# One inverse for four head pairs, recurrences moved beside the projections, and SiLU and GELU as activation functions, in a hybrid block kernel

## The chip, the cores and the metric

The kernel runs on one core of a Trainium2 chip. The metric is the device time of one execution in microseconds; the time of a kernel is the median over its runs.

## The reference

One layer of a decoder trunk, followed by an RMSNorm. x is (1024, 2048), all in float32.

```python
h = rmsnorm(x, ln_g)
proj = h @ w_in                                   # 2048 x 6672, split into eleven segments
out_a = gelu(g_u) * (tril(W_s) layernorm(gelu(g_v)) + b) * silu(g_z)   # 4 groups, chunks of 128
q, k, v = split(silu(causal_conv4([d_q, d_k, d_v])))                   # 8 heads x 128
q, k = l2norm(q) / sqrt(128), l2norm(k)
g = -exp(a_log) * softplus(d_a + dt_bias); beta = sigmoid(d_b)
o = gated_delta_rule(q, k, v, g, beta)            # S_t = a_t (I - b_t k_t k_t^T) S_{t-1} + b_t k_t v_t^T ; o_t = S_t^T q_t
out_b = rmsnorm(o, dn_norm_g) * silu(d_z)
mk, mv = split(rmsnorm(mem) @ w_mem_kv)           # 256 memory tokens, 4 heads
out_c = softmax(c_q mk^T / sqrt(128)) mv * silu(c_z)
y = rmsnorm(x + concat(out_a, out_b, out_c) @ w_out, final_g)
```

The delta rule is computed in chunks; each chunk needs the inverse of a unit lower triangular matrix (I + A).

## The kernel before

**Precision.** A float32 product is made of three matmuls (`triple`): each operand is split into a high part (`hi`, a rounding copy on ScalarE) and a low part (`lo`, a subtraction on VectorE), and hi·hi, hi·lo and lo·hi are accumulated. `split_to` does a split; one weight piece is 128x512, and most splits after the first stage take 128x1024.

**Stages.** After the memory keys and values come the *straight* projections of q, k and v of heads 0 to 3 (`project`, one 128-wide column at a time into one of two accumulator banks): all twelve columns for the first half of the sequence (512 tokens, `hf` 0), then, with the activations reloaded (`refill`), the same twelve for the second half. The remaining columns of `w_in` are made in five *pairs* of 512-wide column blocks (`blocks(0)` to `blocks(4)`, through `project_pair` and `seven`), each with seven block products instead of eight: (q, k of heads 4 to 7), (gates of both sets of heads), (v of heads 4 to 7 and gMLP v), (gMLP u and its gate), (attention gate and query). A product fills four banks (`wide`), in the order 2, 1, 6, 5, 3, 7, 4; each bank is emptied by a copy or an addition. Last come two pairs for the output projection (`out_pair`).

**The delta rule for a pair of heads and a half.** `front` runs two convolutions per head (`conv`: copy the bank to one of three buffers `xr`, three VectorE steps, Tanh) and `qk` (norms, decays, the products for `gt` and `ai`). `blocks_out` writes the 32x32 diagonal blocks of `gt` to DRAM; `inverse` loads them, inverts all of them by 31 dependent steps of two VectorE instructions, and writes the results (`tdr`, `udr`) on ScalarE's DMA queue. `levels` combines the blocks into the full inverse `ut`; `values` convolves v; `back` runs four `scan_step`s and `heads_out`, which leaves the output of heads 0 to 3 in DRAM (`od`). For heads 0 to 3 this is done pair by pair, each of the four with an inverse of its own on 32 partitions: the recurrence of pair 0 and the first half runs in the second half of the straight projections, the next one too, and the last two beside the first pair. For heads 4 to 7 the fronts run beside the second pair and leave q, k, kd, ai (`late_d`) and `gt` (`gt_d`) in DRAM, one inverse on 128 partitions does all four, and `front_late` loads them again for the recurrences, beside the fourth pair and after.

**Order.** All instructions are recorded in a `Plan` and then put in order by a simulation of the engines: an instruction has a class (`rank`, smaller is sooner; 5 if nothing is said, 9 for the large matmuls), an estimated cost, and is issued on its engine when its estimated inputs are ready. The order on each engine and queue is then fixed. Large weight loads, stores and reloads all go through SP's queue.

**What the change touches.** `w_parts` keeps the low parts of eight of the twelve columns in DRAM (`low_d`) in the first half and loads them in the second; `tanh_gate` makes SiLU as (tanh(x/2) + 1) · x with the factor one half put into other constants; `gelu2` makes GELU from Square, Tanh and two VectorE steps; `gate`, `gate_late`, `gmlp_gate` and `attn_gate` apply SiLU to the gate columns, `spatial` and `gmlp` apply GELU. `spatial` takes its values through one bank, `hand`.

Of the kernel before, what the change touches and what calls it, by code (L numbers as in the profile page):

```python
# [9 lines left out]
F32 = mybir.dt.float32  # L10
# [28 lines left out]
GELU_C = math.sqrt(2.0 / math.pi)  # L39
GELU_A = 0.044715  # L40
# [8 lines left out]
class Op:  # L49
    __slots__ = ("eng", "fn", "args", "kw", "cls", "idx", "cost", "lat", "nbytes", "lock", "n", "succ", "ready", "at",  # L50
                 "lead", "tail")
# [11 lines left out]
class Plan:  # L63
# [5 lines left out]
    SWITCH = 250.0  # L69

# [63 lines left out]
    def add(self, eng, name, fn, args, kw):  # L134
        o = Op()
        o.eng, o.fn, o.args, o.kw, o.cls, o.idx = eng, fn, args, kw, self.cls, len(self.ops)
        o.succ, o.n, o.ready = [], 0, 0.0
        outs, ins = [], []
# [83 lines left out]
    def issue(self):  # L222
# [4 lines left out]
        dma = beside = 0.0  # L227
        for o in self.ops:
# [55 lines left out]
def kernel(  # L284
# [377 lines left out]
    V.tensor_scalar(col2[:, 0:8], pt[:, 96:104], 0.25, None, op0=ALU.mult)  # L662
    V.tensor_scalar(col2[:, 8:9], pt[:, 104:105], 0.5, None, op0=ALU.mult)
# [10 lines left out]
    halo = C([P, 24, 3], "halo")  # L674
# [10 lines left out]
    V.tensor_scalar(bsb, bsb, 0.25, None, op0=ALU.mult)  # L685
# [23 lines left out]
    late_d = [[[DT([P, HT], f"late{hf}_{h}_{i}") for i in range(4)] for h in range(NJ)] for hf in range(2)]  # L709
    gt_d = [[DT([P, 2 * HT], f"gtd{hf}_{p}") for p in range(NJ // 2)] for hf in range(2)]  # L710
# [60 lines left out]
    scs = [C([P, 12, NT, NH], f"sc{hf}") for hf in range(2)]  # L771
# [8 lines left out]
    def decays(hf, a):  # L780
# [6 lines left out]
        beta, gg, gc, egl, edk, ngb = (sc[:, i] for i in range(6))  # L787
        w0, w1, w2, w3, w4, egc = (sc[:, i] for i in range(6, 12))
# [42 lines left out]
    low_d, todo = {}, []  # L831
# [59 lines left out]
    def conv(which, h, hf, o, a=None):  # L891
# [3 lines left out]
        if h < NJ:  # L895
# [4 lines left out]
            with rank(1):  # L900
                S.copy(xr[:, 0:3], halo[:, ct])
                S.copy(xr[:, 3:], a)
                if hf == 0:
                    S.copy(halo[:, ct], xr[:, HT:])
                S.activation(o, xr[:, 3:], AF.Copy, scale=w[3])
# [21 lines left out]
    def qk(h, hf, q, k, hs, gt):  # L927

        beta, edk, ngc = (scs[hf][:, i] for i in (0, 4, 6))
        bank = over(scan_banks) if h >= NJ or (h >= NJ - 2 and hf == 1) else tpb  # L930
# [52 lines left out]
    def inverse(gdrs, n, cls):  # L983
# [8 lines left out]
        tmp = (y1 if nr == 32 else y2)[0:nr].rearrange("p c m -> p (c m)")  # L992
# [148 lines left out]
    def front(p, hf, first=(None, None)):  # L1141
# [4 lines left out]
        for i, h in enumerate(hp):  # L1146
# [9 lines left out]
            if h >= NJ:  # L1156
                kd, ai, _ = rest[-1]
                V.tensor_copy(late_hs[:, hf, h - NJ], hs[:, 0:5:4])
                for d, t in zip(late_d[hf][h - NJ], (q, k, kd, ai)):
                    Q.dma_start(d if t.ndim == 2 else tok(d), t)  # L1160
        gdr = blocks_out(gt, f"{hf}{p}")
        if p >= NJ // 2:
            Q.dma_start(gt_d[hf][p - NJ // 2].rearrange("p (h t i) -> p h t i", h=2, i=P), gt)
            return gdr
        return hf, hp, gt, qs, ks, hss, rest, gdr

    def front_late(p, hf, inv):
# [3 lines left out]
        Q.dma_start(gt, gt_d[hf][p - NJ // 2])  # L1171
        qs, ks, hss, rest = [], [], [], []
        for h in hp:
            hss.append(ring["hs"]())
            V.tensor_copy(hss[-1][:, 0:5:4], late_hs[:, hf, h - NJ])
            q, k, kd, ai = (ring[t]() for t in ("qT", "kT", "kd", "ai"))
            for d, t in zip(late_d[hf][h - NJ], (q, k, kd, ai)):
# [3 lines left out]
            rest.append((tok(kd), tok(ai), tok(ring["vs"]())))  # L1181
        return hf, hp, gt.rearrange("p (h t i) -> p h t i", h=2, i=P), qs, ks, hss, rest, inv

    def values(hf, hp, gt, qs, ks, hss, rest, inv):
        for i, h in enumerate(hp):
            v = ring["tn"]()
            conv(2, h, hf, v)
            bank = work() if h >= NJ else scan_banks[i] if h >= NJ - 2 and hf == 1 else tpb()
            by_token(rest[i][2], to_tokens((v, bank))[0], hss[i][:, 4])

    def inverted(n, *states):
        return [(*s[:-1], i) for s, i in zip(states, inverse([s[-1] for s in states], n, 3))]

    def back(hf, hp, gt, qs, ks, hss, rest, inv, ut=None):
        ut = ut or levels(gt, *inv)
# [5 lines left out]
    late_hs = C([P, 2, NJ, 2, NT], "lhs")  # L1201
# [582 lines left out]
```

## Time and profile before

| | |
|---|---|
| median of three runs | 1662.21 us (1661.67 to 1664.04) |
| the profiled execution | 1668.24 us, span 1666.5 us |
| instructions | 26200 |
| DMA | 419.50 MB, mean 252 GB/s |

The span is the time from the first to the last instruction of the profiled execution; the execution's own time is a little longer. Every instruction is recorded through one helper, so the profile gives one line, L280, for all, and groups are told apart by the tiles they write and read. PE is TensorE's matmuls, PEld its weight loads, DVE is VectorE, ACT ScalarE, POOL GpSimd, SP the queue that issues most transfers. `acc` are the banks of the large products, `dn` those of everything else. A matmul's recorded duration overlaps with the next one's, so the rate is read from the starts.

### The profile page before, as it was taken

What the parts mean: (1) busy time and instruction counts of PE and PEld (TensorE: products, weight loads), DVE (VectorE), ACT (ScalarE), POOL (GpSimd) and SP (SyncE); (2) the same over time, 40 slices, a digit from 0 to 9 for tenths busy, and PEclk for the clock granted to TensorE, in tenths of its full rate; (3) what the DMA queues carried; (4) which work ended last, traced back from release to release, by engine and by line L of the source; (5) the groups of instructions that cost most, each with busy time, mean ns of one, the idle gap of its engine ahead of it and who ended that gap; (6) DMA issues with size and microseconds to landing.
All of it is one profiled execution on the core that took longest, in us unless ns stands there. A gap on an engine that the chain in (4) does not pass through costs nothing.

```text
span 1666.5 us, 26200 instructions
## 1 busy us (share of the span) xinstructions
PE 1629.0 (98%) x8570; PEld 1361.7 (82%) x8570; DVE 1322.0 (79%) x2288; ACT 1024.0 (61%) x2235; POOL 133.3 (8%) x171
## 2 busy tenths in 40 slices
PE   8999999899999999999999998999999999999997
PEld 6888887787888888888888887888888888888886
DVE  4865787675887969889999997978767897788875
ACT  5957673575746446876777445776666774345445
POOL 0000200111201000110203001000000000000001
PEclk9999999999999999999999998999999999999999
DMA  7878888685887786679978976898877879689746
GB/s 248 240 236 269 272 282 252 178 255 151 274 260 244 245 269 204 194 256 310 310 234 279 298 222 195 257 309 276 264 249 259 259 265 332 234 274 308 227 138 241
DMA packets 317170, 419.50 MB, mean 252 GB/s; under 512 B 58285, under 2 KB 138854, under 8 KB 317034
## 3 DMA queue, kind: packets, MB, share of 16 engines
q1 hardware_dynamic: 304834, 410.48, 76.4%
q10 hardware_dynamic: 10088, 4.21, 1.0%
q0 software_dynamic: 2112, 3.15, 0.7%
q8 instruction: 67, 1.10, 0.3%
q14 instruction: 69, 0.57, 0.1%
HBM read 334.33 MB, written 82.87 MB: 250 GB/s over the span
## 4 chain that ended last, share of the span: by engine, by line
PE 75%; DMA 6%; DVE 5%; ACT 2%; issue 1%; SPq 1%; ACTq 0%; POOLq 0%; POOL 0%; DVEq 0%
PE acc L280 56%; PE dn L280 18%; DMA wraw<-in_w_in_dram 2%; DVE alo L280 1%; DVE y L280 1%; DMA y<-in_w_in_dram 1%; DVE wlo L280 1%; SPq L280 1%; ACT whi L280 0%; ACT ahi L280 0%; DMA late<-kd 0%; ACTq L280 0%; DMA xr<-pd 0%; DVE zl L280 0%; DVE kT L280 0%
## 5 line engine op out<-in xcount | busy, mean ns | idle before, releaser
L280 PE MATMUL acc<-ahi,whi 128*128 128x512 f32 (+1 forms) x1152 | 454.9, 395 | 13.2 <-ACT xr L280 9.2
L280 PE MATMUL acc<-alo,whi 128*128 128x512 f32 (+1 forms) x1152 | 453.5, 394 | 0.0
L280 PE MATMUL acc<-ahi,wlo 128*128 128x512 f32 (+1 forms) x1152 | 452.2, 394 | 0.2 <-DVE wlo L280 0.2
L280 PEld LDWEIGHTS acc<-ahi,whi 128*128 128x128 f32 x1152 | 218.9, 190 | 57.6 <-ACT xr L280 10.3
L280 PEld LDWEIGHTS acc<-ahi,wlo 128*128 128x128 f32 x1152 | 218.9, 190 | 42.2 <-DVE wlo L280 0.6
L280 PEld LDWEIGHTS acc<-alo,whi 128*128 128x128 f32 x1152 | 218.9, 190 | 40.9
L280 PE MATMUL acc<-ahi,zh 128*128 128x512 f32 x736 | 233.4, 394 | 0.0
L280 ACT CAST whi<-wraw 128x512 fp32r<-128x512 f32 (+1 forms) x170 | 137.2, 808 | 110.2 <-PE acc L280 70.3
L280 DVE TENSOR_TENSOR alo<-raws,ahi 128x1024 fp32r<-128x1024 f32 x131 | 160.1, 1223 | 36.5 <-ACT ahi L280 36.2
L280 ACT CAST ahi<-raws 128x1024 fp32r<-128x1024 f32 x131 | 137.4, 1050 | 74.0 <-PE dn L280 28.2
L280 DVE TENSOR_TENSOR wlo<-wraw,whi 128x1024 fp32r<-128x1024 f32 (+1 forms) x138 | 134.0, 972 | 40.9 <-ACT whi L280 35.5
L280 PEld LDWEIGHTS acc<-ahi,zh 128*128 128x128 f32 x736 | 136.9, 188 | 26.8
L280 PE MATMUL acc<-ahi,zl 128*128 128x512 f32 x368 | 145.1, 394 | 0.0
L280 DVE TENSOR_TENSOR ahi<-y,ahi 128x1024 fp32r<-128x1024 f32 x65 | 79.2, 1219 | 20.9 <-ACT ahi L280 20.9
L280 ACT CAST ahi<-y 128x1024 fp32r<-128x1024 f32 x65 | 68.2, 1050 | 30.7 <-PE acc L280 15.6
L280 PEld LDWEIGHTS acc<-ahi,zl 128*128 128x128 f32 x368 | 69.2, 188 | 13.4
L280 ACT CAST zh<-wraw 128x1024 fp32r<-128x1024 f32 x36 | 37.8, 1050 | 57.3 <-PE acc L280 27.2
L280 POOL TENSOR_TENSOR small<-small,mhalf 128x1 f32<-128x1 f32 x26 | 20.0, 773 | 635.8 <-DVE small L280 619.2
L280 POOL TENSOR_TENSOR hs<-hs,mhalf 128x4 f32<-128x4 f32 x32 | 50.8, 1591 | 236.7 <-DVE hs L280 236.6
L280 PE MATMUL dn<-wlo,ahi 128*128 128x512 f32 x152 | 59.0, 389 | 0.0
L280 PE MATMUL dn<-whi,alo 128*128 128x512 f32 x152 | 59.0, 389 | 0.0
L280 PE MATMUL dn<-whi,ahi 128*128 128x512 f32 x152 | 58.8, 389 | 0.0
(398 smaller groups left out, 3227.5 us busy)
## 6 DMA issues: line engine op xcount, KB each, us to landing
wraw<-in_w_in_dram SPq DMA_DIRECT2D x268, 256.0 KB, 4.1
raws<-sd SPq DMA_DIRECT2D x148, 256.0 KB, 3.7
y<-in_w_in_dram SPq DMA_DIRECT2D x92, 256.0 KB, 4.6
y<-sd SPq DMA_DIRECT2D x77, 256.0 KB, 4.0
wraw<-in_w_out_dram SPq DMA_DIRECT2D x64, 256.0 KB, 4.6
raws<-h0d SPq DMA_DIRECT2D x54, 256.0 KB, 4.3
y<-in_w_out_dram SPq DMA_DIRECT2D x33, 256.0 KB, 4.2
low<-wlo SPq DMA_DIRECT2D x32, 256.0 KB, 4.8
```

What stands on the lines that cost most here:

```text
L280: o.fn(*o.args, **o.kw)
```

## The change

Heads 0 to 3 are now treated as heads 4 to 7 were: fronts first, q, k, kd, ai and also vs to DRAM, one inverse on 128 partitions for all four pair-halves, and the four recurrences beside `blocks(0)`. v of heads 0 to 3 is convolved by `early_values` right after the fronts of each half. The low parts are no longer stored; every piece is split where it is used. SiLU and GELU are single activations, with the constants adapted, and the plan knows three activation tables: a switch is priced at 1.5 us, and an activation of another table counts as 1.5 classes later. The buffers `vks`, `vts` and `tmp` change places.

```diff
+    TABLES = {AF.Exp: "exp", AF.Silu: "silu", AF.Gelu_apprx_tanh: "gelu"}
+    TABLE_LOAD = 1500.0
+    STAY = 1.5
...
-            head = self.ops[heapq.heappop(now[e])[1]]
+            if e == "act":
+                other = [(c + self.STAY * (self.ops[i].table not in (None, table)), i, c) for c, i in now[e]]
+                _, i, c = min(other)
+                now[e].remove((c, i))
+                heapq.heapify(now[e])
+                head = self.ops[i]
+            else:
+                head = self.ops[heapq.heappop(now[e])[1]]
             for o in (head, *head.tail):
                 t = max(t, free[e])
+                if o.table not in (None, table):
+                    t, table = t + self.TABLE_LOAD, o.table
...
-    def tanh_gate(a, o, ts):
-
-        t = ts()
+    def silu(a):
         with rank(1):
-            S.activation(t, a, AF.Tanh, scale=0.5)
-            V.scalar_tensor_tensor(o, t, 1.0, a, op0=ALU.add, op1=ALU.mult)
-
-    def gelu2(a, o, ts):
-
-        t = ts()
+            S.activation(a, a, AF.Silu)
+
+    def gelu(a, o):
         with rank(1):
-            if o is not a:
-                S.copy(o, a)
-            S.activation(t, a, AF.Square)
-        V.scalar_tensor_tensor(t, t, 1.0 / GELU_A, o, op0=ALU.add, op1=ALU.mult)
-        S.activation(t, t, AF.Tanh, scale=GELU_A * GELU_C)
-        V.scalar_tensor_tensor(o, t, 1.0, o, op0=ALU.add, op1=ALU.mult)
+            S.activation(o, a, AF.Gelu_apprx_tanh)
...
     def w_parts(c0, kp):
 
         src = w_in[kp * KP * P : (kp + 1) * KP * P, c0 : c0 + P].rearrange("(k p) c -> p k c", p=P)
-        raw = raw_piece(src)
-        if (c0, kp) in low_d:
-            hi, lo = whi(), wlo()
-            with rank(2):
-                S.copy(hi, raw)
-            with rank(4):
-                Q.dma_start(lo.bitcast(F32), low_d[c0, kp])
-        else:
-            hi, lo = split_piece(raw)
-            if (c0 - C_Q) % DW < 2 * P and c0 < C_DV:
-                return [tok(hi), tok(lo)]
-            low_d[c0, kp] = DT([P, HT], f"low{c0}_{kp}")
-            with rank(6):
-                Q.dma_start(low_d[c0, kp], lo.bitcast(F32))
-        return [tok(hi), tok(lo)]
+        return [tok(t) for t in split_piece(raw_piece(src))]
...
+    def early_values(h, hf):
+
+        v, vs = ring["tn"](), tok(ring["vs"]())
+        conv(2, h, hf, v)
+        by_token(vs, to_tokens((v, tpb()))[0], late_hs[:, hf, h, 1])
+        Q.dma_start(tok(late_d[hf][h][4]), vs)
...
-            q, k, kd, ai = (ring[t]() for t in ("qT", "kT", "kd", "ai"))
-            for d, t in zip(late_d[hf][h - NJ], (q, k, kd, ai)):
+            q, k, kd, ai, vs = (ring[t]() for t in ("qT", "kT", "kd", "ai", "vs"))
+            for d, t in zip(late_d[hf][h], (q, k, kd, ai, vs)):
                 Q.dma_start(t, d)
...
-    state = front(0, 0, (first, None))
-    for u in ring["ut"].bufs:
-        G.memset(u, 0.0)
-    (state,) = inverted("00", state)
-    (ahead,) = inverted("01", front(1, 0))
-    values(*state)
-    values(*ahead)
-    back(*state)
+    gdrs = [front(0, 0, (first, None)), front(1, 0)]
+    for h in range(NJ):
+        early_values(h, 0)
...
-    (state,) = inverted("10", front(0, 1, first))
-    back(*ahead)
-    ut = levels(state[2], *state[-1])
-    values(*state)
-    (ahead,) = inverted("11", front(1, 1))
-    back(*state, ut)
-    values(*ahead)
-    back(*ahead)
+    gdrs += [front(0, 1, first), front(1, 1)]
+    with rank(3):
+        early_inv = inverse(gdrs, "early", 3)
+    for h in range(NJ):
+        early_values(h, 1)
+    for u in ring["ut"].bufs:
+        G.memset(u, 0.0)
...
+    def backs(ps, inv):
+        for hf in range(2):
+            for p in ps:
+                state = front_late(p, hf, inv[hf * 2 + p % 2])
+                ut = levels(state[2], *state[-1])
+                if p >= NJ // 2:
+                    values(*state)
+                back(*state, ut)
+
+    with rank(2.6):
+        backs(range(NJ // 2), early_inv)
     blocks(0, to_conv(0), to_conv(1))
...
     def gate(hf, t, y):
-        tanh_gate(y, y, et)
+        silu(y)
...
-    vts = over(vs01 + ring["E"].bufs)
-    vks = [*halves(ring["gt"]()), steps, states[:, 0:HT]]
+    vts = over(vs01 + [steps, states[:, 0:HT]])
+    vks = [t for u in ring["ut"].bufs for t in halves(u)]
```

More of the change, by code (lines that the diff above doesn't have):

```diff
@@ L137, in add @@
         o.succ, o.n, o.ready = [], 0, 0.0
+        o.table = self.TABLES.get(args[2]) if eng == "act" and len(args) > 2 else None
         outs, ins = [], []
@@ L227, in issue @@
         dma = beside = 0.0
+        table = "exp"
         for o in self.ops:
@@ L786, in decays @@
         sc = scs[hf]
[L787 to L788 removed]
+        beta, gg, gc, egl, edk, ngb, w0 = (sc[:, i] for i in range(7))
+        w1, w2, w3, w4, egc = (sct[:, i] for i in range(5))
         tp = tpb()
@@ L929, in qk @@
         beta, edk, ngc = (scs[hf][:, i] for i in (0, 4, 6))
-        bank = over(scan_banks) if h >= NJ or (h >= NJ - 2 and hf == 1) else tpb
+        bank = over(scan_banks) if h >= NJ else tpb
         qt, kt = to_tokens((q, bank()), (k, bank()))
@@ L1187, in values, with back @@
             conv(2, h, hf, v)
[L1188 to L1195, printed above, removed]
+            by_token(rest[i][2], to_tokens((v, work()))[0], hss[i][:, 4])
+    def back(hf, hp, gt, qs, ks, hss, rest, inv, ut):
         for tt in range(NT):
@@ L1545 @@
     blocks(2, to_conv(2), spatial, dest=lambda hf, t: vks[t])
+    for u in ring["ut"].bufs:
+        G.memset(u, 0.0)
     with rank(2.6):
-        for hf in range(2):
-            for p in range(NJ // 2, NJ):
-                state = front_late(p, hf, late_inv[hf * 2 + p - NJ // 2])
-                ut = levels(state[2], *state[-1])
-                values(*state)
-                back(*state, ut)
+        backs(range(NJ // 2, NJ), late_inv)
     def both(c, j, hf, t, y):
@@ L1639, in attend @@
                 PE.matmul(d, mv[h][:, 1, sl], pT[m][0], start=False, stop=m == 1)
-            S.activation(y, d, AF.Copy, scale=0.5)
+            S.copy(y, d)
             both(1, NG + h, hf, h, y)
     def attn_gate(hf, h, y):
-        tanh_gate(y, y, et)
+        silu(y)
         both(1, NG + h, hf, h, y)
```

60 lines of the change are left out of this document (27 added, 33 removed).

## The prediction

> **What bounds the kernel now.** I read the page first, then TensorE by stage, then TensorE's waits, then the timeline at each wait. From the page:
>
> ```profile
> span 1666.5 us, 26200 instructions
> ...
> PE 1629.0 (98%) x8570; PEld 1361.7 (82%) x8570; DVE 1322.0 (79%) x2288; ACT 1024.0 (61%) x2235; POOL 133.3 (8%) x171
> ```
>
> TensorE is busy in all but 37.5 us of the span, and the change neither adds nor removes a matmul or a transpose. So the change can win only idle time and matmuls run at a lower clock, and lose only by making more of them. Next is the view by stage: columns are the stretch, then busy time of PE, PEld, DVE, ACT and POOL, the granted clock, DMA share and GB/s. The stretches are the first half of the sequence for heads 0 to 3, the second half (in two parts), and the five column pairs.
>
> ```profile
> 84.00:252.00 168.00, 167.88 (x842) 140.55 (x841) 121.38 (x258) 113.36 (x314) 17.43 (x22) 1.00 0.86 265
> 252.00:336.00 84.00, 76.98 (x460) 63.89 (x459) 57.67 (x156) 39.62 (x116) 8.31 (x11) 0.96 0.73 213
> 336.00:426.00 90.00, 86.09 (x517) 72.54 (x516) 57.85 (x143) 58.55 (x173) 13.58 (x15) 0.98 0.67 204
> 426.00:604.00 178.00, 176.34 (x948) 146.79 (x946) 153.38 (x269) 100.71 (x201) 15.81 (x18) 1.00 0.81 259
> 604.00:777.00 173.00, 171.37 (x881) 142.85 (x876) 146.41 (x224) 120.62 (x268) 15.56 (x18) 1.00 0.73 241
> 777.00:941.00 164.00, 162.75 (x771) 134.90 (x770) 150.37 (x252) 114.79 (x247) 30.05 (x33) 1.00 0.86 274
> 941.00:1144.00 203.00, 198.55 (x1206) 166.75 (x1205) 170.85 (x286) 120.93 (x244) 14.11 (x21) 0.97 0.80 253
> 1144.00:1342.00 198.00, 198.00 (x1108) 167.87 (x1108) 155.87 (x255) 134.04 (x305) 7.24 (x8) 1.00 0.80 264
> ```
>
> Three stretches lose something a change here can reach: 252 to 426 (7.02 + 3.91 us idle, clock 0.96 and 0.98) and 941 to 1144 (4.45 us idle, clock 0.97). The other rows lose under 2 us each, and the remaining 17 us of the 37.5 lie before 84 and after 1342, where nothing changes. In TensorE's waits the largest is this one (total, times, longest):
>
> ```profile
> PE acc L280 <- ACT xr L280: 9.2, 3, 3.9
> ```
>
> TensorE cannot start a new weight column because both accumulator banks wait for ScalarE's copy into `xr`. The timelines of TensorE, ScalarE and VectorE around two of the three:
>
> ```profile
> 322.47 0.79 PE L280 MATMUL acc<-ahi,whi 128*128 128x512 f32 x1 [3.69 <-ACT xr L280]
> ...
> 329.08 0.40 PE L280 MATMUL acc<-alo,whi 128*128 128x512 f32 x1
> 329.32 0.39 PE L280 MATMUL acc<-ahi,wlo 128*128 128x512 f32 x1
> ```
>
> ```profile
> 413.25 0.50 PE L280 MATMUL acc<-ahi,whi 128*128 128x512 f32 x1 [3.91 <-ACT xr L280]
> ```
>
> ```profile
> 319.33 0.19 ACT L280 COPY xr<-halo 128x3 f32<-128x3 f32 x1 [1.98 <-DVE kT L280]
> ```
>
> ```profile
> 318.56 0.73 DVE L280 SCALAR_TENSOR_TENSOR kT<-xr,cw,kT 128x512 f32<-128x512 f32 x1
> 319.22 0.35 DVE L280 TENSOR_TENSOR inv<-inv,y 32x207 f32<-32x207 f32 x1
> ```
>
> The copy needs one of three `xr` buffers. They are held by convolutions, whose VectorE steps alternate with the steps of an inverse and of a recurrence (ranks 3 and 1 against the convolution's 5). That is the place where this kernel loses most after its start.
>
> **The stalls of the second half.** The two parts hold 10.93 us of idle time and, by the clock, 0.04 x 76.98 + 0.02 x 86.09 = 4.8 us of slowed matmuls: 15.7 us. The third `xr` wait, near 259 (9.2 less 3.69 and 3.91, so 1.6 us), falls at the change of halves, where weights and activations are reloaded; I count it as staying. That leaves 14.1 us. What is late next there is the same as at 259, a weight piece on its way from DRAM. In the new order no inverse and no recurrence stands beside the q and k columns at all; one inverse remains, beside the v columns of the second half or the start of the first pair. Bounds: all 14.1 us go, or that inverse makes a stall like the one at 413 (3.91 us and the 1.7 us of clock in its part, 5.6) again. I take half of it: 14.1 less 2.8, **-11.3 us**.
>
> **The inverses themselves.** Five chains become two, each of the same 31 steps of two instructions:
>
> ```profile
> L280 DVE TENSOR_TENSOR y<-inv,inv 32x31 f32<-32x31 f32 (+25 forms) x155 | 51.6, 333 | 1.9
> L280 DVE TENSOR_TENSOR inv<-inv,y 32x31 f32<-32x31 f32 (+25 forms) x155 | 51.5, 332 | 1.9
> ...
> L280 DVE SCALAR_TENSOR_TENSOR y<-et,y 128x512 f32<-128x512 f32 x40 | 27.2, 695 | 2.2 <-ACT et L280 2.1
> ...
> L280 ACT COPY y<-acc 128x512 f32<-128x512 f32 x72 | 41.9, 584 | 12.3 <-PE acc L280 12.0
> ...
> L280 ACT ACTIVATE et<-y 128x512 f32<-128x512 f32 x40 | 24.8, 631 | 10.7 <-DVE y L280 10.4
> ...
> L280 DVE TENSOR_TENSOR wlo<-kT,whi 128x512 fp32r<-128x512 f32 x14 | 9.6, 688 | 6.7 <-ACT whi L280 4.9 <-PE acc L280 1.9
> ```
>
> (51.6 + 51.5) x 3/5 = 61.9 us leave VectorE; it is worth only what the stalls above are worth, so nothing more is counted. What the combined inverse adds is its end: eight writes in a row on ScalarE's queue, where single ones stood before. The late inverse shows the price:
>
> ```profile
> 1000.33 4.13 ACTq L280 DMA_DIRECT2D tdrlate<-inv  x4
> ...
> 1004.81 5.26 ACTq L280 DMA_DIRECT2D udrlate<-inv  x4
> ```
>
> ```profile
> 1012.79 0.50 PE L280 MATMUL acc<-ahi,whi 128*128 128x512 f32 x1 [1.48 <-ACT y L280]
> ...
> 1015.80 2.08 PE L280 MATMUL dn<-wsT,el 128*128 128x128 f32 x8 [2.03 <-ACT et L280]
> ```
>
> ScalarE issues for 9.4 us; queued behind the issues are its casts of the next operands and the bank copies, and soon after TensorE waits 1.48 us for bank copies and 2.03 us for the GELU that holds bank `hand`. The stretch loses 4.45 us and 0.03 x 198.55 = 6.0 us of clock, 10.4 us. In the first pair there is no `hand` and the writes may fall between two rounds of bank copies: between 0 and 10.4 us, I take **+3**, nearer to none, because the copies come only every 22 us or more.
>
> **Low parts no longer kept.** 32 stores and 32 loads leave SP's queue; 32 subtractions of 0.688 us come to VectorE, 22 us, all in the second half. VectorE was busy 57.67 + 57.85 of 174 us there, and two inverses (41 us) leave it, so the cover is there: **0**. If the cover were gone, it would show as `wlo` late.
>
> **Through DRAM, and the recurrences moved.** Heads 0 to 3 now store q, k, kd, ai, vs (40 stores) and four `gt`, and load them again in the first pair, on SP, between weight loads; a store that waits for its data holds up the weight loads behind it. SP's 64 issues for low parts go. From 604 to 777 the fronts of heads 4 to 7 store in the same way, at 1.63 us idle: that is the upper bound. The recurrences take the same TensorE time in another place. That a pair can hide four of them is seen late in the kernel: they run from the first to the last row here, across two stretches of which the second is busy 198.00 of 198.00 us at 264 GB/s.
>
> ```profile
> 1018.24 1.06 PE L280 MATMUL dn<-tblk,gt 32*32 32x32 f32 x32
> ```
>
> ```profile
> L280 ACT ACTIVATE vs<-dn,col x16: 678/682/691, 337.2 to 1269.8; 128x512 f32<-128x512 f32 x16
> ```
>
> ```profile
> L280 SPq DMA_DIRECT2D od<-vs x8: 319/320/349, 337.9 to 675.9; - x8
> ```
>
> 1269.8 - 1018.2 = 252 us for four, to the last head's output. The early ones ended at 675.9, when the last output left for DRAM (tile `od`). Two recurrences out of the second half and the stalls bring the start of the first pair to about 385; the inverse then ends near 415, and 415 + 252 = 667, no later than now. Then the fronts of heads 4 to 7, which follow on the same buffers, start no later: **0**; a gain is excluded, as TensorE's work is the same.
>
> **SiLU and GELU.** The 40 steps of 0.695 us above belong to 32 SiLUs and 8 GELUs. Each SiLU loses that step and keeps one activation; each of the 16 GELUs goes from two activations to one and loses two VectorE steps. Of the 2.03 us wait at 1015.80 for a GELU half should go: **-1** (bounds 0 and -2). Against that stand table loads:
>
> ```profile
> L280 ACT ACT_TABLE_LOAD x1 | 1.3, 1283 | 4.2 <-DMA y<-in_mem_norm_g_dram 4.2
> ```
>
> Today there is one, so Tanh, Exp, Square and Copy share a table; that Silu or Gelu shares it with Exp isn't shown, and the planner now prices switches. Activations come in groups of four, one group for each finished product. Second pair: four SiLU groups between exponentials of the fronts, 8 loads; third: two GELU groups, 4; fourth: GELU, SiLU, SiLU, GELU, 4; fifth: two SiLU groups among the softmax, 8. I estimate 24 loads, 31 us of ScalarE, against 490 busy of 738 us from 604 to 1342. A finished bank must be emptied before the next product's first six matmuls on it, and those of the other three banks come between: 18 x 0.23 = 4.1 us. A load, a SiLU and a copy are 1.28 + 0.63 + 0.58 = 2.5 us and fit. Bounds: 0, or all 31 us. The block of 9.4 us above cost 3.5 us of idle, a third, but it was seven loads long; I take a tenth: **+3**.
>
> The Trainium skill, "ScalarE: Activation LUTs", section "What ACT_TABLE_LOAD costs", adds a drain of about 1.38 us to each load, 2.66 us in all. By that, an estimate, 24 loads would be 64 us of ScalarE and the tenth 6 us instead of 3. The row here shows only the 1.28 us; no row shows the drain.
>
> **Sum.** -11.3 + 3 + 0 + 0 - 1 + 3 = -6.3 us. The profiled execution took 1668.2 us, 1.7 more than its span; 1661.9 after. The median of the runs, 1662.2, lies 6.0 below the profiled one, so the time predicted is 1655.9.
>
> **Rivals.**
> - *Everything hides.* The inverse meets no full `xr` ring, the writes fall between copies, and the lighter GELU frees the stretch at 1012: -14.1 - 10.4 = -24.5, 1637.7. For it: no wait of TensorE stands between 1144 and 1342 though all engines are loaded. Against: something else is usually late next, and 9.4 us of ScalarE issues remain at the late inverse.
> - *Given back.* The combined inverse repeats a stall (+2.8 more), and its writes cost their full price (+7.4 more): -6.3 + 10.2 = +3.9; with either one alone within 0.2% of today, about 1660. The same holds if the plan places the early recurrences no earlier than the pair's end.
> - *Table loads between bank copies (slower).* SiLU has rank 1 and the fronts' exponentials rank 2.6; whenever ScalarE has nothing else ready it takes an exponential and switches, and the next SiLU switches back. Two loads for each of 32 SiLUs are 82 us. Two loads, the SiLU, the copy and one split of 1.05 us are 5.3 us against the 4.1: 1.2 us idle each, 38 us if always, and about 25 if two in three fall so: -11.3 + 3 + 25 = +16.7, 1679. It decides once more than about 15 switches stand ahead of a due copy. For it: ScalarE is at 70% there (120.62 of 173), the copies stand in its order behind whatever is ready. Against: the planner prices each switch at 1.5 us and avoids it by rank. The Trainium skill, same page, section "Rules for kernel authors", says to do all of one set before switching; this kernel interleaves them, so that rule speaks for this rival. The trace has one load and can't yet bear it out.
>
> **How the numbers follow.** Forecast 0.44; everything hides 0.14; given back 0.14; table loads 0.28. About 0.2% (3.3 us) is what a measurement of this kernel can tell from no change. Faster: 0.44 + 0.14 = 0.58; within: 0.12 of "given back"; slower: 0.28 + 0.02 = 0.30. The range leaves out the better half of the first rival and the worst third of the last: 1640 to 1677. The forecast's own range, with its unknown costs, is 1648 to 1660.
>
> **What would show it.** Right: no `xr` wait of TensorE over 1 us before the first pair, clock 1.00 there; inverse rows x62 each instead of x155; about 24 table loads; recurrences done by about 665; TensorE's busy time lower by the slowed matmuls alone. Wrong: table loads well over 40 with TensorE waiting for `y` or `xr` behind them; new waits on `wlo` or `wraw` in the second half; the fronts of heads 4 to 7 starting later than now.

## The result, and the profile after

| | before | after |
|---|---|---|
| median of 12 runs each | 1664.45 us | 1661.49 us |
| profiled execution, span | 1668.24, 1666.5 us | 1662.46, 1660.7 us |

The ratio is 0.9987, 95% interval 0.9974 to 1.0001: about 2 us less, not clear of no change. The profiled pair lies 5.8 us apart, because the profiled execution of before is 3.8 us above the median of its twelve runs and that of after 1.0 above. Ratios below are all to the kernel before.

The page of after, span and busy time per engine:

```profile
span 1660.7 us, 26037 instructions
...
PE 1623.1 (98%) x8570; PEld 1357.9 (82%) x8570; DVE 1253.7 (75%) x2081; ACT 1027.4 (62%) x2226; POOL 109.2 (7%) x166
```

VectorE lost 68 us and the time hardly moved. By stage (stretch, then busy time of PE, PEld, DVE, ACT, POOL, the clock, DMA share, GB/s):

```profile
252.00:336.00 84.00, 83.77 (x402) 69.55 (x401) 62.16 (x134) 54.52 (x149) 5.91 (x7) 1.00 0.80 239
336.00:426.00 90.00, 89.04 (x409) 73.27 (x408) 74.47 (x147) 50.97 (x114) 13.37 (x23) 1.00 0.91 297
426.00:604.00 178.00, 171.96 (x1185) 145.30 (x1184) 107.19 (x164) 94.24 (x224) 7.91 (x15) 0.98 0.82 269
...
941.00:1144.00 203.00, 196.16 (x1210) 165.16 (x1209) 150.78 (x247) 121.69 (x250) 10.67 (x18) 0.98 0.80 256
```

From 252 to 426 TensorE now loses 0.23 + 0.96 = 1.2 us where it lost 15.7: the stalls went. From 426 to 604 it loses 6.04 us of idle time and 0.02 x 171.96 = 3.4 us of clock, 9.5, where it lost 1.66. From 941 to 1144: 6.84 + 3.9 = 10.8 us, as before (10.4). From 1342 to 1640 TensorE is idle 2.6 us where before it wasn't idle at all. TensorE's idle time over the whole span is the same as before (37.6 us, before 37.5): it stands in other places. TensorE's two longest waits are new ones, and the `xr` wait is gone from the head of the list:

```profile
PE dn L292 <- DVE el L292: 6.8, 1, 6.8
PE acc L292 <- DVE y L292: 5.0, 1, 5.0
```

Their places, in the timelines of TensorE and of ScalarE (start, duration; in brackets idle time before and what ended it):

```profile
441.28 1.19 PE L292 MATMUL acc<-ahi,zh 128*128 128x512 f32 x2 [4.96 <-DVE y L292]
...
1009.10 2.08 PE L292 MATMUL dn<-wsT,tn 128*128 128x128 f32 x8 [6.83 <-DVE el L292]
```

```profile
425.95 1.71 ACTq L292 DMA_DIRECT2D tdrearly<-inv  x3
428.78 5.05 ACTq L292 DMA_DIRECT2D udrearly<-inv  x3
435.37 0.31 ACTq L292 DMA_DIRECT2D tdrearly<-inv  x1
436.09 0.31 ACTq L292 DMA_DIRECT2D udrearly<-inv  x1
436.50 1.04 ACT L292 CAST ahi<-y 128x1024 fp32r<-128x1024 f32 x1 [10.15 <-DMA udrearly<-inv]
...
989.05 3.73 ACTq L292 DMA_DIRECT2D tdrlate<-inv  x4
995.51 6.34 ACTq L292 DMA_DIRECT2D udrlate<-inv  x4
1001.95 0.62 ACT L292 CAST whi<-kT 128x512 fp32r<-128x512 f32 x1 [12.15 <-DMA tblk<-tdrlate]
```

ScalarE runs nothing from 426.3 to 436.5: eight writes stand ahead of its next cast. The first two lines that matter on VectorE in the same stretch:

```profile
437.57 1.22 DVE L292 TENSOR_TENSOR ahi<-y,ahi 128x1024 fp32r<-128x1024 f32 x1 [7.56 <-ACT ahi L292]
...
440.45 1.28 DVE L292 TENSOR_TENSOR y<-acc,y 128x512 f32<-128x512 f32 x2
```

VectorE's next instruction needs that cast and waits 7.56 us for it; behind it in VectorE's order stand the additions that empty the banks, so TensorE, out of banks at 436.3, waits until 441.28. The same happens at 989 to 1002, where VectorE waits 9.08 us. So about half of the gain at the stalls was given back at the end of the early inverse; the end of the late one costs what it did before.

### The profile page after: what moved, and what is told of

Its sections match the earlier page's. It is cut to its first block, busy times and chain, and to the rows that moved or that the text cites. A ratio compares the mean times of both kernels' runs of the same rounds, so it can differ in the third digit from the quotient of the medians.

```text
span 1660.7 us, 26037 instructions
## 1 busy us (share of the span) xinstructions
PE 1623.1 (98%) x8570; PEld 1357.9 (82%) x8570; DVE 1253.7 (75%) x2081; ACT 1027.4 (62%) x2226; POOL 109.2 (7%) x166
## 4 chain that ended last, share of the span: by engine, by line
PE 82%; DMA 7%; DVE 5%; ACT 2%; issue 2%; SPq 0%; ACTq 0%; DVEq 0%; POOLq 0%; POOL 0%
PE acc L292 62%; PE dn L292 21%; DMA wraw<-in_w_in_dram 2%; DVE wlo L292 1%; DMA wraw<-hTd 1%; DMA wraw<-in_w_out_dram 1%; DVE alo L292 1%; ACT whi L292 1%; DMA y<-in_w_in_dram 1%; DVE y L292 0%; SPq L292 0%; ACTq L292 0%; DMA hTd<-tn 0%; ACT ahi L292 0%; DVE wraw L292 0%
## 5 line engine op out<-in xcount | busy, mean ns | idle before, releaser
L292 PE MATMUL acc<-ahi,zh 128*128 128x512 f32 x736 | 237.1, 399 | 6.0 <-DVE y L292 5.0
L292 DVE TENSOR_TENSOR wlo<-wraw,whi 128x512 fp32r<-128x512 f32 (+1 forms) x170 | 157.3, 926 | 73.9 <-ACT whi L292 64.5
L292 ACT CAST zh<-wraw 128x1024 fp32r<-128x1024 f32 x36 | 37.8, 1050 | 42.2 <-PE acc L292 25.2
L292 DVE TENSOR_TENSOR zl<-wraw,zh 128x1024 fp32r<-128x1024 f32 x36 | 43.9, 1220 | 21.5 <-ACT zh L292 21.3
L292 POOL TENSOR_TENSOR small<-small,mhalf 128x1 f32<-128x1 f32 x26 | 17.1, 662 | 627.7 <-DVE small L292 627.7
```

The source lines that it names most:

```text
L292: o.fn(*o.args, **o.kw)
```

## The experiments: the ends of the two inverses

**Writes on GpSimd's queue, on SP's queue, or spread.** Three versions of after:

```diff
-                flat(S.dma_start, tdr[i], ti[i * 32 : (i + 1) * 32])
-                flat(S.dma_start, udr[i], gd[i * 32 : (i + 1) * 32])
+                flat(G.dma_start, tdr[i], ti[i * 32 : (i + 1) * 32])   # e2; Q in e1; e3: S, rank(3) for rank(1)
+                flat(G.dma_start, udr[i], gd[i * 32 : (i + 1) * 32])
```

> The changed kernel with one edit: the eight DMA writes at the end of each inverse (tdr, udr) go out on POOL's queue instead of ScalarE's. Theory 'held queue': what the removed stalls gained is given back at the ends of the two 128-partition inverses, where ScalarE stands behind its own writes for 10 and 12 us; in the changed kernel's trace that costs 4.96 us idle and 2.17 us of clock at 434, and 6.83 us idle and 3.0 us of clock at 994 to 1022, 16.9 us in all. Then both waits go and the time falls from 1661.5 to about 1645. Rival 'late anyway': VectorE and the operands are behind by then whatever ScalarE does, the waits stay or move: 1657 to 1664.

> The changed kernel with the same eight writes on SP's queue, among the weight loads. 'Held queue': ScalarE runs on, but SP may be held instead and the weight loads behind the writes come late; between 1645 (SP has slack) and 1661 (the stall changes its name to wraw). If the writes issue in well under 10 us there, the hold belongs to ScalarE's queue and not to the DMA engines. 'Late anyway': 1657 to 1664 with the same waits for VectorE.

> The changed kernel with the writes left on ScalarE's queue but with rank 3 instead of 1, so that casts (rank 2) and bank copies (rank 1) that are ready go ahead of each of them. 'Held queue': each write still takes its 1.2 to 1.6 us, but the operands' slack of some us takes them one by one; most of the 16.9 us go, about 1649. 'Late anyway': 1657 to 1664. If the writes still stand in a row, because nothing else is ready by the plan, no change either, and the run tells nothing.

GpSimd: 1654.32 us, ratio 0.994 [0.9924, 0.9956], between its theory (1645) and its rival (1657 to 1664). SP: 1658.51, 0.9966 [0.9955, 0.9977]. Spread: 1661.52, 0.9976 [0.9961, 0.9991], not clear of after. Four of the eight late writes on SP, and on GpSimd (duration least, median, largest; first and last start):

```profile
L292 SPq DMA_DIRECT2D tdrlate<-inv x4: 364/412/425, 998.9 to 1000.3; - x4
```

```profile
L292 POOL DMA_DIRECT2D udrlate<-inv x4: 489/489/489, 995.1 to 997.5; - x4
```

The hold of ScalarE is its queue's; with the spread writes it stays (TensorE idle 4.5 us at 434 to 448). By stage, most of what e2 wins lies at the late inverse, where before lost as much as after: TensorE is busy 203.00 of 203 us from 941 to 1144, where after lost 10.8. On SP too only the late end gains (1.2 us lost there, 10.0 in the first pair). In e2's first pair 7.6 of the 9.5 us stay, 4.14 of them idle, in three pieces between 450 and 457:

```profile
426.00:604.00 178.00, 173.86 (x1201) 147.52 (x1200) 106.95 (x164) 99.76 (x234) 11.24 (x21) 0.98 0.83 276
```

That has another cause; in the same run, SP's queue and then VectorE:

```profile
441.11 2.18 SPq L292 DMA_DIRECT2D tblk<-tdrearly  x4
443.64 2.17 SPq L292 DMA_DIRECT2D ut<-udrearly  x4
445.86 0.93 SPq L292 DMA_DIRECT2D tblk<-tdrearly  x2
446.84 4.07 SPq L292 DMA_DIRECT2D ut<-udrearly  x8
451.00 0.85 SPq L292 DMA_DIRECT2D wraw<-in_w_in_dram  x2
```

```profile
453.78 0.69 DVE L292 TENSOR_TENSOR wraw<-wraw,y 128x512 f32<-128x512 f32 x1 [5.49 <-DMA wraw<-in_w_in_dram]
```

The first recurrence's reads of the inverted blocks fill SP's queue for 10 us, and the next weight load leaves at 451.00.

**The same in the kernel before.** All inverse writes of before on GpSimd (the same two lines):

> The kernel before with the writes of all its inverses on POOL's queue. 'Held queue': only the late inverse has eight in a row; 4.45 us idle and 4.1 us of clock between 1008 and 1050 go, the three xr stalls stay: 1664.5 - 8.6 = 1656. 'Late anyway': within 2 us of 1664.5.

1667.33, 1.0015 [1.0003, 1.0027], above both its theory and its rival. With the clock, the gap at the late inverse shrank from 8.6 to 3.7 us, but the stall at 406 grew from 5.1 to 9.7. Why that stall grew isn't shown. So removing the hold wins nothing there.

**The reads of the blocks.** After with GpSimd's writes, and the reads of `tblk` and `ut` on GpSimd too (e4), or on SP at rank 5, behind the weight loads (e5); and e5's reads with the writes left on ScalarE (e7):

```diff
-            Q.dma_start(dst, src[b * NB : (b + 1) * NB][e].rearrange("c i j -> i c j"))
+            with rank(5):
+                Q.dma_start(dst, src[b * NB : (b + 1) * NB][e].rearrange("c i j -> i c j"))
```

> The changed kernel with the inverse's writes on POOL's queue (as in e2_pool) and also its block reads (tblk, ut: 48 for each set of four) on POOL's queue instead of SP's. With the writes moved, 4.14 us idle and 2.4 us of clock remained at 448 to 460: SP issues 18 block reads at rank 1 from 441 to 451, and the next weight load leaves at 451. Theory 'held queue, the second one': weight loads then leave in time, the stall goes, and 1654.3 - 6.5 = 1648, 1646 to 1651. Rival: POOL's reads are slower and the recurrences, or the stall of the output stage (5.7 us at 1414), take it back: 1653 to 1658.

> As e2_pool, but the block reads stay on SP's queue with rank 5, behind weight loads (rank 4) that are ready. 'Held queue, the second one': the reads go out between weight loads, the stall at 448 shrinks, 1648 to 1652, the recurrences start some us later without cost. If ready weight loads are few at that moment by the plan, the reads still stand in a row, and it stays at 1654.

> The kernel after with the reads of inverted blocks (tblk, ut) at rank 5 on SP, so behind the weight loads, and the inverse's writes left on ScalarE's queue. Theory (two holds, each with its own place): the reads' hold of SP at the early inverse goes and ScalarE's hold of about 10 us at each inverse stays, so this gives only its own part: 1655 to 1660 us, ratio 0.994 to 0.997, TensorE still idle 3 to 6 us near 994. Rival (one hold): the reads wait for the writes, so later reads free everything, as with the writes on GpSimd: 1646 us, ratio 0.990. Rival (ScalarE alone): reads matter only once the writes are off ScalarE: 1661, ratio 0.998 to 1.000.

e4: 1652.26, 0.9942 [0.9921, 0.9963], no better than the writes alone: its first pair loses 3.9 us instead of 7.6, but 777 to 941 loses 3.2 instead of 0.8. e5: **1645.8, 0.99 [0.9883, 0.9916]**, faster than both kernels and than its theory had it. e7: 1663.38, 0.9995 [0.9983, 1.0008], nothing: the gap at 434 stays (5.2 us and the clock), as its last rival had it. The two holds stand in a row: the reads matter only once the writes are off ScalarE. In e5 the first pair loses 2.1 us, near the 1.66 of before, in one wait for a cast on ScalarE:

```profile
426.00:604.00 178.00, 175.87 (x1215) 148.93 (x1214) 113.44 (x174) 97.02 (x229) 12.97 (x24) 1.00 0.85 283
```

**Early or late.** Only the early inverse's writes on GpSimd (f2), only the late one's (f3):

```diff
-                flat(S.dma_start, tdr[i], ti[i * 32 : (i + 1) * 32])
+                flat((G if n == "early" else S).dma_start, tdr[i], ti[i * 32 : (i + 1) * 32])   # "late" in f3; udr alike
```

> The kernel after with the eight writes of the early inverse alone on GpSimd's queue. Theory (the end of the early inverse costs about 7 us, but SP's reads of the blocks take its place): the gap at 434 becomes one of 4 to 6.5 us at 448, and only 1 to 3 us are won: 1658 to 1660, ratio 0.997 to 0.998. Rival (the early end alone explains what the writes cost): 1654, ratio 0.994.

> The kernel after with the eight writes of the late inverse alone on GpSimd's queue. Theory: the late end's hold of ScalarE (10 us of idle time and slow clock at 994 to 1022) goes and nothing is late behind it: 1654 to 1657, ratio 0.994 to 0.9965. Rival: a late hold only puts off what is late anyway: 1660, ratio 0.998 to 0.9995.

f2: 1654.18, 0.995 [0.9933, 0.9966]; f3: 1655.43, 0.9951 [0.9934, 0.9967]. f3's time is as its theory had it, though 4.7 us are still lost from 941 to 1144; f2's time is its rival's, yet its trace isn't:

```profile
426.00:604.00 178.00, 175.39 (x1209) 149.17 (x1208) 108.48 (x165) 99.95 (x234) 11.28 (x21) 0.98 0.84 277
941.00:1144.00 203.00, 202.37 (x1248) 170.74 (x1247) 159.49 (x257) 122.71 (x243) 10.14 (x17) 1.00 0.84 266
```

The early stretch still loses 2.6 + 3.5 = 6.1 us, so 3.4 less than after, near the 1 to 3 of the theory. The late one loses 0.6 us though its writes are still on ScalarE: in this plan they fall where nothing waits. The late end's price thus depends on where the plan puts the writes, and the two savings don't add. Every edit also makes the plan sort all instructions anew, so a run can win or lose some us in stretches that its edit doesn't touch (e4 and f2 above, p4 below).

## The experiments: the three parts taken apart

The change has three parts: the new order (one inverse, through DRAM, recurrences beside the first pair, with its buffers), no kept low parts, and activations. Six versions complete the table of eight. Parts are undone by restoring, or done by taking over, the lines of the diff, the planner's table prices going with the activations where these were added to before.

```diff
 # p1: after, activations undone; p3: this and the next
-        silu(y)
+        tanh_gate(y, y, et)
-            gelu(hand, v)
+            gelu2(hand, v, et)
 # p2: after, low parts kept again
+            low_d[c0, kp] = DT([P, HT], f"low{c0}_{kp}")
+            Q.dma_start(low_d[c0, kp], lo.bitcast(F32))
 # b2, b3, b4: the kernel before with the first pair of lines reversed, with the second taken out, with both
```

> The changed kernel with SiLU and GELU again from Tanh, Square and VectorE steps, with the constants that go with them; no table is switched. The changed kernel's trace has 15 loads beyond the first, and no wait of TensorE over 0.6 us within some us of one. Theory 'off the path': the activations are worth nothing either way, 1661.5 within 2.5 us, and the stall at the end of the late inverse (near 1000, 9.8 us with its clock) is there as before, with the GELU's wait for bank hand in it (about 2 us). Rival 'loads cost': without them 1655 to 1658. Rival 'loads gain': the lighter gates were what kept the second pair clear, 1666 or more.

> The changed kernel with both the activations and the stored low parts of the kernel before: only the heads through DRAM, the one inverse and the moved recurrences remain. If this part alone carries the change: the xr stalls between 250 and 440 are gone (14.6 us with their clock in the trace), the end of the early inverse costs about 8, so 1664.5 - 6.6 = 1658, 1656 to 1661. If the low parts or the activations carried part of it: 1663 or more.

> The kernel before with SiLU and GELU as activations (and the plan's prices of table switches) alone. Theory (shared VectorE): the 40 saved VectorE steps are worth about 23 us in the new structure because there the fronts of heads 4 to 7, one inverse and the late recurrences wait in line for VectorE; in the order of before, the last late recurrence starts before the fifth pair anyway, so the same edit is worth little: 1650 to 1664 us, ratio 0.993 to 1.001, with the VectorE steps of the late inverse ending 5 to 15 us sooner than 1000. Rival (own worth): the edit saves 23 us wherever it stands: 1639 us, ratio 0.986. Rival (table loads): ScalarE's loads cost here what other things hid there: ratio above 1.003.

> The kernel before with no low parts kept in DRAM, all pieces split where they are used. Theory (shared VectorE): in the order of before, five inverses and two recurrences share VectorE with the straight projections, so the 32 more subtractions (22 us) lengthen the xr stalls between 252 and 440 by 3 to 10 us, while the transfers that go save less: 1662 to 1674 us, ratio 1.000 to 1.007. Rival (own worth): keeping low parts costs about 26 us wherever it is done, so dropping them gives 1636 us, ratio 0.984.

> The kernel after, with the low parts of eight of the twelve columns stored and loaded again as before; the new order and the activations stay. Theory: the stored low parts cost in the new order because the transfers of q, k, kd, ai and vs stand on the same SP queue between their loads: the parts add, and the time is 1685 us (1710.4 less 23 to 26; ratio 1.012 to 1.016), with TensorE waiting over 10 us in all between 224 and 448, on ACT ahi, DVE tn and the loads of wlo. Rival (only with the VectorE load): the loss of 26 us came from both together, and with activations the low parts cost under 5 us: 1661 to 1667, ratio below 1.003.

> The kernel before with both smaller parts of the change (SiLU and GELU as activations, no low parts kept) and its order as it was; it differs from the kernel after by the new order alone. Theory (the parts depend on each other): in the order of before the activations gave -4 us and dropping the low parts +9, and the two touch different stretches, so they add: 1663 to 1671 us, ratio 1.000 to 1.0045; the new order is then worth -2 to -8 us once both are in, against +48 us with neither. Rival (the two also hang together): with the activations in, VectorE has room for the 32 subtractions, and the kernel is at 1655 us or less, ratio 0.995 or below; the new order then costs time even in the finished change.

| ratio to before [95%] | old order | new order |
|---|---|---|
| low parts kept, Tanh | 1 | 1.0292 [1.0274, 1.031] (p3) |
| low parts kept, activations | 0.9976 [0.9964, 0.9989] (b2) | 1.0174 [1.0156, 1.0191] (p2) |
| none kept, Tanh | 1.0052 [1.0037, 1.0067] (b3) | 1.0139 [1.0119, 1.0158] (p1) |
| none kept, activations | 1.0055 [1.0039, 1.007] (b4) | 0.9987 [0.9974, 1.0001] (after) |

No part has a price of its own. The new order costs 2.9% with neither of the others and wins 0.7% (11 us) with both. Activations are worth 0.2% alone in the old order and 1.5% (25 us) in the finished change. Dropping the low parts costs 0.5% in the old order and wins 1.9% (31 us) in the finished change. p1 and p3, the first two, missed by far: 1684.51 us where 1659 to 1664 was expected, with its rival "loads gain" right at least in direction, and 1710.36 where 1656 to 1661 would have shown that the order alone carries the change. The times of b2 and b3 lie in the ranges of their theories (b2's late inverse writes 19 us sooner, more than the 5 to 15 expected); p2 and b4 came just above the range of theirs (in the old order the activations gave nothing more once the low parts were dropped), and their rivals fell.

Why dropping them costs in the old order, from the waits of b4 between 200 and 470:

```profile
PE acc L294 <- ACT xr L294: 12.8, 3, 7.9
```

The 32 subtractions come to VectorE while the inverses still stand beside the convolutions: it is 65.67 + 65.87 us busy from 252 to 426 instead of 57.67 + 57.85, and the `xr` stalls grow from 9.2 to 12.8 us. With the clock, the two stretches lose 24.3 us instead of 15.7.

Why keeping them costs in the new order, from the stages of p2:

```profile
252.00:336.00 84.00, 79.07 (x369) 64.39 (x367) 48.67 (x107) 48.28 (x131) 4.63 (x5) 1.00 0.89 271
336.00:426.00 90.00, 76.96 (x331) 61.71 (x331) 49.88 (x107) 43.59 (x116) 14.27 (x24) 0.92 0.90 300
```

VectorE is idle for nearly half of it, and the DMA engines are at 0.89 and 0.90 instead of the 0.73 and 0.67 of before (after: 0.80 and 0.91). The largest of TensorE's waits between 200 and 470 is for a kept low part:

```profile
PE acc L292 <- DMA wlo<-low: 4.8, 2, 3.6
```

The loads of kept low parts take longer from issue to landing (last number, us), in before and in p2:

```profile
wlo<-low SPq DMA_DIRECT2D x32, 256.0 KB, 4.0
```

```profile
wlo<-low SPq DMA_DIRECT2D x32, 256.0 KB, 5.8
```

**Transfers or SP's queue?** p4 is p2 with the low parts' stores and loads on GpSimd's queue:

```diff
-                Q.dma_start(lo.bitcast(F32), low_d[c0, kp])
+                G.dma_start(lo.bitcast(F32), low_d[c0, kp])     # and the store alike
```

> The kernel after with the low parts stored and loaded again, as in the run that kept them (ratio 1.0174), but on GpSimd's queue instead of SP's. Theory (transfers): in the new order the DMA engines are 0.89 to 0.90 busy from 252 to 426 with the low parts on top, the loads of wlo land 5.8 us after their issue instead of 4.0, and another queue does not add capacity: 1685 to 1695 us, ratio 1.013 to 1.019, stalls between 364 and 448 as large. Rival (order on SP): the loads wait behind stores of q, k, kd, ai and vs that wait for their data, so with a queue of their own most of the 32 us goes: 1663 to 1675, ratio 1.000 to 1.007.

1679.66, 1.0102 [1.0082, 1.0122], between the two. By stage:

```profile
252.00:336.00 84.00, 80.88 (x376) 65.72 (x375) 50.28 (x110) 49.25 (x133) 13.56 (x21) 1.00 0.92 287
336.00:426.00 90.00, 76.00 (x336) 60.87 (x335) 52.80 (x113) 44.16 (x119) 22.42 (x40) 0.92 0.93 295
426.00:604.00 178.00, 173.06 (x1176) 145.13 (x1175) 114.03 (x174) 97.68 (x210) 7.72 (x14) 0.99 0.83 273
```

From 252 to 426 the loss is that of p2 (17.1 us of idle time against 18.0): there SP's order isn't the cause. The nearest reading is that the transfers are too many, whatever queue issues them: `wlo` lands after 6.0 us in p4, and at 383.80 ScalarE has waited 7.77 us for a weight piece. It isn't isolated, and the mean share alone doesn't explain it: after stands at 0.91 from 336 to 426 and is idle 0.96 us there. By slices of 12 us, p4 is at 0.95 or more for 72 us in a row (324 to 396), after for 36 (336 to 372). After 426 TensorE is busy 173.06 of 178 us in p4 instead of p2's 169.17; but p4 wins most from 941 to 1144, where no low part moves (0.5 us lost instead of 10.8), probably by where its plan puts the late inverse's writes, as in f2. How much of the 12 us between p4 and p2 was SP's order isn't shown.

## The experiments: why activations are worth 25 us in the new order

In p1 VectorE is busy 1291.3 us instead of 1253.7 and the late inverse's writes start at 1065 instead of 989; afterwards TensorE waits at their end and for the last recurrence. The reading to be tried: the fronts of heads 4 to 7 share VectorE with SiLU and GELU and come late. To tell VectorE's time from everything else, after got multiplications by 1.0 on VectorE, in place:

```diff
             S.activation(a, a, AF.Silu)
+            V.tensor_scalar(a, a, 1.0, None, op0=ALU.mult)      # twice in f4
...
             S.activation(o, a, AF.Gelu_apprx_tanh)
+        V.tensor_scalar(o, o, 1.0, None, op0=ALU.mult)
+        V.tensor_scalar(o, o, 1.0, None, op0=ALU.mult)
```

> The kernel after with its single activations, and behind each SiLU one and behind each GELU two multiplications by 1.0 on VectorE in place, so VectorE's 64 steps of the kernel before come back without Tanh and Square. Theory (VectorE's load): what the activations save in the new order is VectorE's time beside the second and third pair; the late inverse ends at 1020 to 1065 instead of 989, TensorE waits again near 1020 to 1080 and 1260 to 1290, and the time is 1672 to 1685 us, ratio 1.006 to 1.014. Rival (ScalarE's work and the constants): the saving came from ScalarE or the other edits, and the 64 steps hide: 1661 to 1664, ratio below 1.001.

> As the run that put multiplications by 1.0 behind SiLU and GELU (64 steps, 20 us of VectorE, ratio 1.0023), with two of them behind each SiLU: 96 steps of 0.42 us, 41 us, as much as the VectorE time that the activations save (1291.3 less 1253.7 is 37.6). Theory (VectorE's load, growing faster than in proportion once the fronts of heads 4 to 7 fall behind): the late inverse's writes start at 1030 or later (989 after, 1001 with 64 steps, 1065 without activations), and the time is 1675 to 1688 us, ratio 1.008 to 1.015. Rival (the load is the smaller part, the rest is ScalarE's order with Tanh and Square): in proportion, 1.0023 + 0.0036 is 1.006 or less, 1668 to 1672 us, the late inverse's writes before 1020.

f1 (20 us more of VectorE): 1666.12, 1.0023 [1.001, 1.0035]. f4 (35 us more, 1289.0 in all): 1705.24, 1.0263 [1.0244, 1.0281]. The first writes of the late inverse (first and last start), in after, f1, p1 and f4:

```profile
L292 ACTq DMA_DIRECT2D tdrlate<-inv x4: 312/317/397, 989.1 to 992.5; - x4
```

```profile
L292 ACTq DMA_DIRECT2D tdrlate<-inv x4: 309/376/434, 1001.3 to 1005.2; - x4
```

```profile
L294 ACTq DMA_DIRECT2D tdrlate<-inv x4: 309/398/727, 1065.2 to 1069.3; - x4
```

```profile
L292 ACTq DMA_DIRECT2D tdrlate<-inv x4: 308/376/1766, 1100.6 to 1106.5; - x4
```

TensorE's waits from 1050 to 1310 have the same names in p1 and in f4:

```profile
PE acc L294 <- DVE y L294: 8.7, 1, 8.7
PE dn L294 <- DVE steps L294: 7.4, 2, 5.6
PE dn L294 <- ACT vs L294: 4.0, 3, 3.4
```

```profile
PE acc L292 <- DVE y L292: 13.5, 1, 13.5
PE dn L292 <- ACT vs L292: 7.9, 6, 5.2
PE dn L292 <- DVE steps L292: 6.3, 2, 6.1
```

f1 lies between its theory and its rival, f4 beyond its theory. So more steps on VectorE, with nothing else undone, are enough to bring p1's loss and its waits, and they cost out of proportion: the first 20 us cost 0.36% (6 us), the next 15 another 2.4% (39 us). What comes late are the fronts: their last diagonal blocks leave for DRAM (`gdr`) at 888.9 in after, 900.9 in f1, 975.5 in p1 and 1018.7 in f4. Yet from 604 to 1000 VectorE is about equally busy in all four (343, 343, 353 and 341 of 396 us): in this stretch the added steps take the fronts' place in its order and don't fill idle time. That f4 loses more than p1 with no more VectorE time was not expected; its steps stand in other places than those they replace, and their time and their place in the order were not separated.

## Why the prediction was wrong, point by point

- **The sum.** -6.3 us was forecast, a clear gain; the runs show about -2, as in the rival "given back" with one of its two parts. Idle time and clock by stage give: stalls -14.5, first pair +7.8, late inverse +0.3, the rest +3, in all -3.4. The rest (2.6 after 1342, 1.1 from 84 to 252) had no term in the forecast. The other 2.4 us between the two spans can't be placed: the clock is given to two digits, up to 0.9 us in a stretch of 178, and each profile is of one execution.
- **The step that failed: the end of the combined inverse**, +3 with bounds 0 and 10.4. It measured +7.8, TensorE idle 4.96 us at 441 with the clock down behind it. That "the writes may fall between two rounds of bank copies" looked at the wrong wait: what stood behind them was a cast of the next operand, which holds VectorE and so the banks, and casts come far more often than every 22 us (the two before the writes start at 420.76 and 425.29). With +7.8 the sum would have been -1.5. The mechanism itself (issues ahead of ScalarE's work) is the one that was named, but a second hold behind it, the reads of the blocks on SP, was not priced at all: without the writes on ScalarE the first pair still lost 7.6 us (e2), with the reads later too 2.1 (e5). The 0.47% that e2 won came mostly from the late inverse.
- **Stalls of the second half**, -11.3: -14.5. The forecast that no inverse beside the columns means no `xr` stall held; the 1.6 us that I left standing at the change of halves went too. The half of a stall kept for the one inverse did not come there.
- **Low parts, 0.** Wrong as a price of its own: +0.5% in the old order, where the 41 us of two inverses had not left; and in the new order a gain of 31 us against keeping them. I looked for VectorE's cover and not at the transfers: the new order raises the DMA share from 0.73 and 0.67 to 0.80 and 0.91 even without the low parts. That the transfers are the cause fits p2 and p4 but isn't isolated.
- **Through DRAM and the recurrences moved, 0.** True only with the other two parts in: otherwise the order costs 0.9% to 2.9%. The early recurrences ended sooner, as forecast: the last output left at 665.5 (forecast 667, before 675.9).
- **SiLU and GELU, -1.** Sized by one wait for a GELU; in the new order, it is with the steps they take off VectorE that the fronts and the late inverse come in time. And the stretch at 1012 lost as much as before, though the GELU is single.
- **Table loads, +3, and the slower rival.** There are 16 loads with the first, where 25 were estimated, and none of the 15 others is followed by a wait of TensorE over 0.6 us within 5 us. The rival's sum was also wrong: two loads, the SiLU, the copy and the split are 4.8 us by their rows, not 5.3, so 0.7 us over the 4.1 each time and about 1669 instead of 1679. Term and rival both fall:

```profile
L292 ACT ACT_TABLE_LOAD x16 | 20.5, 1283 | 4.3 <-DMA y<-in_mem_norm_g_dram 4.0
```

```profile
643.39 0.72 ACT L292 ACTIVATE kT<-xr,cw 128x512 f32<-128x512 f32 x1
644.12 1.28 ACT L292 ACT_TABLE_LOAD   x1
645.42 0.63 ACT L292 ACTIVATE y<-y 128x512 f32<-128x512 f32 x1
```

A load stands 1.31 us between the end of one activation and the start of the next. The Trainium skill, "ScalarE: Activation LUTs", section "What ACT_TABLE_LOAD costs", gives the same 1283 ns and a drain of 1.38 us more: the trace agrees with the first and shows no second one.

- **VectorE's 61.9 us** of inverse chains, taken as worth only the stalls: the groups are as forecast, 62 steps of each kind (`inv<-inv,y`: 20.9 us, where it was 51.5).

## What to carry to other kernels

A sum of parts holds only if each part is priced in the kernel that has the others: here neither the order, nor the low parts, nor the activations had a price of its own. When many small steps are joined into one, look at what is issued at its end and on which engine's queue: here the writes at the ends of the two inverses, moved to an engine with little other work (GpSimd, 7% busy), and their readers put behind the weight loads, turned a change of no clear worth into 1% off the kernel before. Where two holds stand in a row, undoing the second alone shows nothing.

## What the hardware showed that was not expected

Eight writes of 128 KB take ScalarE's queue 10.5 to 12.8 us, though each is recorded with only about 0.31 us: they start up to 3.1 us apart and ScalarE runs nothing between. On SP the same eight take 4 to 6 us, on GpSimd 4 to 5, mostly 0.49 us each. The Trainium skill, "DMA: Bandwidth & Descriptors", section "Issuing engines are not separate DMA queues", says that issuing from several engines saves only the sequencer's time, usually small: p4 agrees from 252 to 426, where another queue changed little (17.1 us idle, p2 18.0). The writes of the inverses don't: 10.5 to 12.8 us on one queue, 4 to 6 on the others. What keeps ScalarE's issues apart isn't shown.
